# A hybrid decoder step: tensor arithmetic moved off GpSimd, modulation pieces used in pairs, another order at the end of the kernel

## The chip, the cores and the metric

The kernel runs on one NeuronCore of a Trainium2 chip. A core has five engines with queues of their own: TensorE (PE in the profile: matmuls; PEld: its weight loads), VectorE (DVE), ScalarE (ACT), GpSimd (POOL) and SyncE (SP, which here only issues DMAs). Each engine works through its queue in order and waits on semaphores of the others. The metric is the device time of one launch in microseconds (us), median of several runs.

## The reference, cut to what matters

One inference step of a decoder layer, for 256 prompt tokens and 8 sample tokens with states of their own:

```
mod = silu(c) @ w_mod + b_mod                       # 2048 -> 6 x 2048, for 9 conditions
h = rmsnorm(x, g_mix) * (1 + sc_m) + sh_m
u_a, u_b, v_b, z, xbc, dt, gates = split(h @ w_in)
o_a = s5_branch(u_a)         # diagonal complex SSM, scan over tokens, GELU, GLU
o_b = gmlp_branch(u_b, v_b)  # causal 128x128 spatial weights per head, masked
o_c = ssd_branch(z, xbc, dt) # causal conv, Mamba-2 chunked scan with masked scores, gated norm
merged = sum of sigmoid(gate) * (o @ w_p), over a, b, c
x = x + gt_m * (merged @ w_out)
h2 = rmsnorm(x, g_ffn) * (1 + sc_f) + sh_f
up = causal_conv3(h2 @ w_up);  x = x + gt_f * ((silu(up_a) * up_b) @ w_down)
y = rmsnorm(x, g_final)
```

All states at the end of the sequence and of the sample tokens are outputs too.

## The kernel before, in words

Activations lie feature-major: 128 features on the partitions, and T = 264 tokens (256 + 8) in the free dimension. Every weight matrix is streamed from HBM once, in pieces of 512 KB (four k-tiles of 128 by 256 columns, 128x1024 in SBUF). To keep fp32 accuracy, each piece is split (`load_w`, L287): ScalarE rounds it to `hi`, and a subtraction makes the residue `lo` = raw - hi. A gemm of one piece (`gemm_piece`, L308) is 24 matmuls of 128x264: hi by the activation's hi, hi by its lo, and lo by its hi. The residue is made on VectorE, but for some pieces on GpSimd: every third of the first two k-steps (L1130, 6 pieces), and every second of the streams in `SHARED` (L31, L1143: `w_pb`, `w_ga`, `w_pa`, `w_z`, 32 pieces). `raw` has 3 buffers, `hi` and `lo` 4 each; `take` keeps up to three pieces ahead. SP's queue holds all weight loads in order, and the load of a piece waits until the raw buffer's former piece has been read by both engines.

The input projection is done in five k-steps (`KSTEPS`: 2, 2, 4, 4, 4 k-tiles): during each step the modulation of the next one's features is computed (`mod_gen`, L358), since a k-tile can be modulated as soon as its shift and scale are there. Those matmuls use 32 of TensorE's 128 columns each, in one of four column groups (`tile_position`, c = k % 4), and read pieces of 512 KB; in the steps of four k-tiles a piece holds two k's, and the generator loads and uses pieces two at a time. Two consecutive pieces so serve the four column groups.

Work beside the gemms sits in generators: `fill` (S5 preparation and tables, gMLP, SSD), advanced by `pump` by a credit in us for each piece, where each `yield` gives an estimate of the work it emitted, and `mods`, advanced by `mpump`. `finish` drains a generator at once. A planner then orders each engine's instructions by this order of emission and by its own cost model; what is marked high priority goes ahead. On the chip the order of each engine is fixed.

`gen_s5_tables` (L629) builds four tables of cosine and sine by seven doublings each, six GpSimd instructions a doubling; their first reader is the S5 scan (`gen_s5`), which starts at about 340 us. GpSimd also applies three causal or block masks (L781, L948, L1026 to L1030), and issues output DMAs and small DRAM round trips. `rstd_tok` (L490) makes a row of 1/rms for all tokens: three sums, a short chain on VectorE with one square root on ScalarE, three scaled diagonals `dg` on VectorE, and a matmul by ones that broadcasts them to PSUM (`rsb`).

At the end, `residual` (L1331) handles each 256-column group of `w_down`; in the last group each half is squared and summed by its own three matmuls. Then `rstd_tok`, and `final` (L1430) multiplies each piece of the output by the row: some on VectorE from PSUM, some on VectorE and two on GpSimd from a copy in SBUF (`rsb`), and sends it out.

Of the kernel before, what the change touches and what calls it, by code (L numbers as in the profile page):

```python
# [23 lines left out]
NB = 8  # L24
# [6 lines left out]
SHARED = ("w_pb", "w_ga", "w_pa", "w_z")  # L31
# [164 lines left out]
def build(tc, I, O):  # L196
# [62 lines left out]


# [26 lines left out]
    def load_w(src, kk, n, e=V):  # L287
# [5 lines left out]
        sub(lo, raw, hi.bitcast(F32), e)  # L293
# [39 lines left out]
    def mod_part(sec, i, nk, raw):  # L333
        if i == 0:
            mod_ps[sec] = PM("mod")
        ps = mod_ps[sec]
        for j in range(8 // nk):
            k = 8 // nk * i + j
            c = k % 4
            mm(ps[32 * c:32 * c + 32, :128 * nk], cs[:, k, :], raw[:, j, :], k < 4, k >= KD - 4,  # L340
               tile_position=(0, 32 * c))

    def mod_fin(sec, k0, n):
        ps = mod_ps.pop(sec)
# [13 lines left out]
    def mod_gen(s_, k0, nk, depth):  # L358
# [4 lines left out]
        for j in range(len(steps) + depth):  # L363
# [126 lines left out]
    def rstd_tok(pt, PM=PM, n=D):  # L490
# [10 lines left out]
        ts(dg[:, :128], ident, r[:, 0:1], ALU.mult)  # L501
# [127 lines left out]
    def gen_s5_tables():  # L629
        co, si = trig[:, 0], trig[:, 1]  # L630
        tt = W("tt", [P, 512]).rearrange("p (a s m) -> p a s m", a=2, s=4)
        for u in range(4):
            tab = Q1k("tab").rearrange("p (a s t) -> p a s t", a=2, s=4)
            tc_, ts_ = tab[:, 0], tab[:, 1]
            tabs[u] = (tc_, ts_)
            V.memset(tc_[:, :, 0:1], 1.0)
            V.memset(ts_[:, :, 0:1], 0.0)
            e = G
            for b in range(7):
                m = 2 ** b  # L640
                cb = co[:, b, 4 * u:4 * u + 4].unsqueeze(2).to_broadcast([P, 4, m])
                sb = si[:, b, 4 * u:4 * u + 4].unsqueeze(2).to_broadcast([P, 4, m])
# [134 lines left out]
    def gen_gm(ub, vb):  # L777
# [3 lines left out]
        G.affine_select(out=w3, in_=w3, compare_op=ALU.is_ge, fill=0.0, base=0,  # L781
                        pattern=[[0, 8], [1, 128]], channel_multiplier=-1)
# [113 lines left out]
    def gen_ssd(raws):  # L896
# [567 lines left out]
```

## Time and profile before

| | |
|---|---|
| median of 3 runs | 1696.12 us (1695.43 to 1696.61) |
| the profiled execution | 1694.82 us |
| its span, first to last instruction | 1692.8 us |
| mean granted TensorE clock | 0.984 of full speed |
| the chain that ended last | PE 86%, DVE 8%, DMA 2%, ACT 2%, issue 1% |
| DMA | 385.13 MB, mean 228 GB/s |

The busy time of an engine is the union of its instructions' spans; instructions overlap a little in an engine's pipeline, so that the starts of consecutive ones lie closer than their durations. A wait is put down to the producer that came last. The granted clock has two levels, 1.0 (2.4 GHz) and 0.5 (1.2 GHz); a value between is a mean over the stretch. The chain of work that ended last runs through TensorE's gemms for nearly its whole length, so the time is TensorE's work plus the gaps in it.

### The profile page before, as it was taken

The numbers are of one execution on the slowest core, as the hardware profiler recorded it, in microseconds if no ns is written. First come the engines' busy times: TensorE is split into PE (matmuls) and PEld (weight loads), VectorE is DVE, ScalarE is ACT, GpSimd is POOL, SyncE is SP. The second block draws the span as 40 slices with busy tenths as digits, with TensorE's granted clock in tenths as the row PEclk, the third lists the DMA queues.
The fourth block names the chain that finished last, engine by engine and source line by source line (L and its number), as shares of the span: only waits on it lengthen the run. The fifth ranks groups of instructions, "written<-read, shape, count | busy, mean of one in ns | idle before, by whom it ended". The sixth has DMA issues, their size and how long they took to land.

```text
span 1692.8 us, 32239 instructions
## 1 busy us (share of the span) xinstructions
PE 1641.0 (97%) x13175; PEld 1515.9 (90%) x13175; DVE 1098.5 (65%) x1817; ACT 799.7 (47%) x1166; POOL 201.0 (12%) x252
## 2 busy tenths in 40 slices
PE   8999999989988999999999999999999999999996
PEld 6678899877967899879989999999999999999996
DVE  3456877599987658675547666666545566666554
ACT  4423346534345779644335444545333445455442
POOL 0200069133332320000000000000000000000000
PEclk8999999999999999999999999999999999999998
DMA  8867885766477659768996666555555555555552
GB/s 322 299 239 286 339 290 174 284 211 242 174 272 275 224 198 322 258 218 298 337 329 200 229 219 224 175 174 189 184 179 182 180 181 186 178 186 180 186 178 98
DMA packets 107268, 385.13 MB, mean 228 GB/s; under 512 B 12192, under 2 KB 13408, under 8 KB 107120
## 3 DMA queue, kind: packets, MB, share of 16 engines
q1 hardware_dynamic: 103968, 372.58, 63.1%
q0 software_dynamic: 3152, 10.50, 1.7%
q8 instruction: 103, 1.69, 0.4%
q14 instruction: 45, 0.37, 0.1%
HBM read 374.56 MB, written 8.46 MB: 226 GB/s over the span
## 4 chain that ended last, share of the span: by engine, by line
PE 86%; DVE 8%; DMA 2%; ACT 2%; issue 1%; SPq 0%; DVEq 0%; ACTq 0%
PE pg L258 79%; PE mods L258 3%; PE mod L258 2%; DVE lo L243 1%; DVE cv L246 1%; DVE s5b L237 1%; DVE s5gr L737 1%; ACT hi L255 1%; DMA raws<-in_w_mod 1%; DVE s5gi L737 1%; DMA raw<-in_w_pc 0%; DVE s5b L240 0%; DVE s5b L243 0%; PE ypy L258 0%; DMA cT<-in_c 0%
## 5 line engine op out<-in xcount | busy, mean ns | idle before, releaser
L243 DVE TENSOR_TENSOR lo<-raw,hi 128x1024 fp32r<-128x1024 f32 x457 | 568.1, 1244 | 418.6 <-ACT hi L255 401.8
L255 ACT ACTIVATE hi<-raw 128x1024 fp32r<-128x1024 f32 (+1 forms) x495 | 520.4, 1054 | 647.0 <-PE pg L258 495.5
L258 PE MATMUL pg<-hh,hi 128*128 128x264 f32 x1408 | 399.5, 284 | 0.0
L258 PE MATMUL pg<-hh,lo 128*128 128x264 f32 x1408 | 399.3, 284 | 0.0
L258 PE MATMUL pg<-hl,hi 128*128 128x264 f32 x1408 | 398.4, 283 | 0.0
L258 PE MATMUL pg<-xh,hi 128*128 128x264 f32 x1296 | 373.9, 289 | 4.7 <-ACT xh L255 2.5
L258 PE MATMUL pg<-xh,lo 128*128 128x264 f32 x1296 | 369.7, 286 | 1.9 <-DVE lo L243 1.8
L258 PE MATMUL pg<-xl,hi 128*128 128x264 f32 x1296 | 369.0, 285 | 0.0
L258 PEld LDWEIGHTS pg<-xh,hi 128*128 128x128 f32 x1296 | 244.5, 189 | 37.5 <-issue 17.9
L258 PEld LDWEIGHTS pg<-hh,hi 128*128 128x128 f32 x1408 | 264.5, 188 | 10.9 <-issue 9.2
L258 PEld LDWEIGHTS pg<-hl,hi 128*128 128x128 f32 x1408 | 264.4, 188 | 0.0
L258 PEld LDWEIGHTS pg<-hh,lo 128*128 128x128 f32 x1408 | 264.3, 188 | 0.0
L258 PEld LDWEIGHTS pg<-xh,lo 128*128 128x128 f32 x1296 | 243.9, 188 | 8.6 <-issue 4.8
L258 PEld LDWEIGHTS pg<-xl,hi 128*128 128x128 f32 x1296 | 244.4, 189 | 5.2 <-issue 4.9
L258 PE MATMUL pg<-fl,hi 128*128 128x264 f32 x704 | 199.6, 284 | 0.0
L258 PE MATMUL pg<-fh,hi 128*128 128x264 f32 x704 | 199.4, 283 | 0.0
L258 PE MATMUL pg<-fh,lo 128*128 128x264 f32 x704 | 199.3, 283 | 0.0
L258 PEld LDWEIGHTS pg<-fh,hi 128*128 128x128 f32 x704 | 132.4, 188 | 0.0
L258 PEld LDWEIGHTS pg<-fh,lo 128*128 128x128 f32 x704 | 132.4, 188 | 0.0
L258 PEld LDWEIGHTS pg<-fl,hi 128*128 128x128 f32 x704 | 132.3, 188 | 0.0
L243 POOL TENSOR_TENSOR lo<-raw,hi 128x1024 fp32r<-128x1024 f32 x38 | 99.6, 2622 | 274.9 <-ACT hi L255 230.9
L246 DVE SCALAR_TENSOR_TENSOR fcv<-pg,par,fcv 128x255 f32<-128x255 f32 (+1 forms) x176 | 83.9, 477 | 1.5 <-ACT fcv L255 1.5
(346 smaller groups left out, 1990.9 us busy)
## 6 DMA issues: line engine op xcount, KB each, us to landing
raw<-in_w_up SPq DMA_DIRECT2D x176, 512.0 KB, 3.5
raws<-in_w_mod SPq DMA_DIRECT2D x128, 512.0 KB, 5.9
raw<-in_w_down SPq DMA_DIRECT2D x88, 512.0 KB, 3.5
raw<-in_w_a SPq DMA_DIRECT2D x64, 512.0 KB, 5.2
rawm<-in_w_m SPq DMA_DIRECT2D x64, 512.0 KB, 7.0
raw<-in_w_ga SPq DMA_DIRECT2D x32, 512.0 KB, 3.8
raw<-in_w_gc SPq DMA_DIRECT2D x32, 512.0 KB, 5.0
raw<-in_w_out SPq DMA_DIRECT2D x32, 512.0 KB, 4.6
```

Source lines behind the costliest of these rows:

```text
L237: e.tensor_tensor(o, a, b, op=ALU.mult)
L243: e.tensor_tensor(o, a, b, op=ALU.subtract)
L246: V.scalar_tensor_tensor(o, a, s, b, op0=op0, op1=op1)
L255: S.activation(o, a, f, **kw)
L258: TE.matmul(o, l, r, start=start, stop=stop, skip_group_check=True, **kw)
L737: V.tensor_tensor_scan(g[:, s, k], rb, b[:, s, k], ini[:, 4 + r, s:s + 1] if c else 0.0, op0=ALU.mult, op1=ALU.add)
```

## The change

- `load_w` always makes the residue on VectorE; `SHARED` and the choice of engine are gone.
- `gen_s5_tables` does cosine and sine in one instruction each time, four instructions a doubling in place of six, on VectorE; the estimates given to `pump` go from 0.2 a doubling to 0.7 to 1.7 (6.7 a table).
- The masks become products with `tri` on VectorE; the masked scores `CB` are read from PSUM by that product, so ScalarE's copy goes. In the decode part the block matrix `E` and its eight matmuls are replaced by two small products with strided columns of `ident` and two matmuls by `ones` in two column groups.
- `mod_gen` uses the two pieces of a pair in the reverse order of their loading; `mod_part` counts per column group which matmul is the first and the last, since the order is no longer that of k.
- `rstd_tok` makes the first of the three diagonals on ScalarE.
- In the last group the two squares are added on VectorE and summed by three matmuls once. Twelve matmuls of 256 columns on zeros, whose result nobody reads, are queued behind them. The output is sent in eight parts, with five multiplications and two fused ones on VectorE that read the row in PSUM, and two on GpSimd.

```diff
-    def load_w(src, kk, n, e=V):
+    def load_w(src, kk, n):
...
-        sub(lo, raw, hi.bitcast(F32), e)
+        sub(lo, raw, hi.bitcast(F32))
...
     def mod_part(sec, i, nk, raw):
-        if i == 0:
-            mod_ps[sec] = PM("mod")
-        ps = mod_ps[sec]
+        if sec not in mod_ps:
+            mod_ps[sec] = PM("mod"), [0] * 4
+        ps, seen = mod_ps[sec]
         for j in range(8 // nk):
             k = 8 // nk * i + j
             c = k % 4
-            mm(ps[32 * c:32 * c + 32, :128 * nk], cs[:, k, :], raw[:, j, :], k < 4, k >= KD - 4,
+            seen[c] += 1
+            mm(ps[32 * c:32 * c + 32, :128 * nk], cs[:, k, :], raw[:, j, :], seen[c] == 1, seen[c] == KD // 4,
                tile_position=(0, 32 * c))
...
-                for p_, raw in enumerate(got.popleft()):
+                for p_, raw in reversed(list(enumerate(got.popleft()))):
                     mod_part(sec, i + p_, nk, raw)
...
-        ts(dg[:, :128], ident, r[:, 0:1], ALU.mult)
+        act(dg[:, :128], ident, AF.Copy, scale=r[:, 0:1])
...
-                t1, t2 = tt[:, 0, :, :m], tt[:, 1, :, :m]
-                mult(t1, ts_[:, :, :m], sb, e)
-                mult(t2, ts_[:, :, :m], cb, e)
-                mult(tc_[:, :, m:2 * m], tc_[:, :, :m], cb, e)
-                mult(ts_[:, :, m:2 * m], tc_[:, :, :m], sb, e)
-                sub(tc_[:, :, m:2 * m], tc_[:, :, m:2 * m], t1, e)
-                add(ts_[:, :, m:2 * m], ts_[:, :, m:2 * m], t2, e)
-                yield 0.2
+                t, new = tt[:, :, :, :m], tab[:, :, :, m:2 * m]
+                mult(t, tab[:, :, :, :m], sb)
+                mult(new, tab[:, :, :, :m], cb)
+                sub(new[:, 0], new[:, 0], t[:, 1])
+                add(new[:, 1], new[:, 1], t[:, 0])
+                yield (0.7, 0.7, 0.7, 0.8, 0.9, 1.2, 1.7)[b]
...
-        G.affine_select(out=w3, in_=w3, compare_op=ALU.is_ge, fill=0.0, base=0,
-                        pattern=[[0, 8], [1, 128]], channel_multiplier=-1)
+        mult(w3, w3, tri.unsqueeze(1).to_broadcast([P, 8, 128]))
...
-        act(CB, pt.rearrange("p (c g i) -> p c g i", c=2, g=2), AF.Copy)
-        CBf = CB.rearrange("p c g i -> p (c g) i")
-        G.affine_select(out=CBf, in_=CBf, compare_op=ALU.is_ge, fill=0.0, base=0,
-                        pattern=[[0, 4], [1, 128]], channel_multiplier=-1)
+        mult(CB.rearrange("p c g i -> p (c g) i"), pt.rearrange("p (c i) -> p c i", c=4),
+             tri.unsqueeze(1).to_broadcast([P, 4, 128]))
...
-        for t in range(8):
-            mm(pe[:, 16 * t:16 * t + 16], E[:16, 128 * t:128 * t + 128], ddf, True, True)
+        for o in range(2):
+            mm(pe[64 * o:64 * o + 64, :128], ones[:16, :64], ddm[:, o].rearrange("p t c -> p (t c)"), True, True,
+               tile_position=(0, 64 * o))
...
-                if end:
-                    sum_tok(sst[0], [t[:, 0, :]], False, j0 == 1)
+                if not end:
+                    add(ssq, ssq, t)
+                elif j0 == 0:
+                    t0 = t
                 else:
-                    add(ssq, ssq, t)
+                    add(t, t, t0)
+                    sum_tok(sst[0], [t[:, 0, :]], False, True)
...
+    wps = PG()
+    with tc.issue_after(newest(TE)):
+        for _ in range(12):
+            mm(wps[:, 0, :256], wsrc[:, :128], wsrc, True, True)
     rs = rstd_tok(sst[0])
+    rsb = W("rsb", [P, T])
+    act(rsb, rs, AF.Copy)
...
     final(0, h0, rs, V)
-    rsb = W("rsb", [P, T])
-    act(rsb, rs, AF.Copy)
     final(1, h0, rsb, G)
     final(0, h1, rs, V)
-    final(2, slice(0, 4), rsb, V)
+    final(2, h0, rs, V)
+    final(2, h1, rs, V)
     final(1, h1, rsb, G)
-    mult(x1[3][:, h0, :], x1[3][:, h0, :], rsb.unsqueeze(1).to_broadcast([P, 2, T]))
-    for j in (2, 3):
-        stt(x1[3][:, j, :], x1[3][:, j, :], pv("g_final", 12 + j, 13 + j), rsb, ALU.mult, ALU.mult)
-    nc.sync.dma_start(O["y"][3], x1[3])
+    final(3, h0, rs, V)
+    final(3, h1, rs, V, True)
```

## Rows read from the trace of the kernel before

**Rows 1.** The page's busy time of each engine: us, share of the span, instructions

```profile
PE 1641.0 (97%) x13175; PEld 1515.9 (90%) x13175; DVE 1098.5 (65%) x1817; ACT 799.7 (47%) x1166; POOL 201.0 (12%) x252
```

**Rows 2.** TensorE's waits: waiting group, releaser, us in total, times, longest

```profile
PE rsb L258 <- DVE dg L250: 8.9, 2, 7.0
PE mods L258 <- DMA raws<-in_w_mod: 5.6, 4, 3.8
...
PE pg L258 <- ACT xh L255: 2.5, 1, 2.5
```

**Rows 3.** Windows: us, busy time by engine, TensorE's clock, DMA share, GB/s

```profile
60.00:70.00 10.00, 7.49 (x42) 4.53 (x41) 7.81 (x14) 4.69 (x8) 2.46 (x1) 0.83 0.94 327
...
180.00:190.00 10.00, 10.00 (x81) 8.04 (x81) 9.93 (x38) 3.19 (x4) 0.00 (x0) 1.00 1.02 391
...
215.00:297.00 82.00, 82.00 (x677) 80.81 (x676) 61.02 (x95) 43.17 (x50) 72.70 (x168) 1.00 0.69 232
297.00:340.00 43.00, 43.00 (x367) 37.35 (x359) 22.54 (x38) 22.18 (x30) 8.16 (x6) 1.00 0.79 282
...
335.00:560.00 225.00, 207.23 (x1581) 172.54 (x1580) 195.84 (x331) 97.66 (x151) 72.16 (x32) 0.95 0.66 239
```

**Rows 4.** GpSimd's residues, groups of instructions, 335 to 560 us

```profile
L243 POOL TENSOR_TENSOR lo<-raw,hi 128x1024 fp32r<-128x1024 f32 x25 | 68.3, 2732 | 147.1 <-ACT hi L255 134.4 <-PE mods L258 12.7
```

**Rows 5.** Timeline of VectorE and GpSimd: start us, us, engine, line, instruction

```profile
30.00 0.17 DVE L237 TENSOR_TENSOR hd<-hd,rstd 128x16 f32<-128x16 f32 x1
...
61.14 2.35 DVE L237 TENSOR_TENSOR hd<-x,gs 128x16 f32<-128x16 f32 x1
...
106.30 0.42 DVE L243 TENSOR_TENSOR lo<-raw,hi 128x256 fp32r<-128x256 f32 x1
...
334.53 0.28 DVE L237 TENSOR_TENSOR s5d<-h0s,a_i 128x128 f32<-128x128 f32 x1
...
344.40 2.40 POOL L243 TENSOR_TENSOR lo<-raw,hi 128x1024 fp32r<-128x1024 f32 x1 [5.04 <-PE mods L258]
344.46 0.70 DVE L237 TENSOR_TENSOR acc<-acc,pg 128x528 f32<-128x528 f32 x1
345.07 2.27 DVE L240 TENSOR_TENSOR s5b<-s5b,s5gi 128x512 f32<-128x512 f32 x1
347.26 0.68 DVE L243 TENSOR_TENSOR s5b<-s5b,s5gr 128x512 f32<-128x512 f32 x1
...
556.09 2.41 DVE L240 TENSOR_TENSOR cv<-cv,pre 128x32 f32<-128x32 f32 x1
```

**Rows 6.** VectorE's residues of whole pieces, 215 to 297 and 730 to 890 us

```profile
L243 DVE TENSOR_TENSOR lo<-raw,hi 128x1024 fp32r<-128x1024 f32 x27 | 35.5, 1315 | 9.7 <-ACT hi L255 9.7
...
L243 DVE TENSOR_TENSOR lo<-raw,hi 128x1024 fp32r<-128x1024 f32 x47 | 57.5, 1224 | 49.9 <-ACT hi L255 48.0 <-PE mods L258 1.6
```

**Rows 7.** Windows of TensorE, modulation matmuls alone: busy (records), clock, DMA

```profile
60.00:112.00 52.00, 16.68 (x68) 0.97 0.69 249
...
157.00:215.00 58.00, 8.10 (x64) 1.00 0.84 309
```

**Rows 8.** Timeline: a broadcast at 889 us, and the end

```profile
889.20 0.71 PE L258 MATMUL rsb<-dg,ones 128*128 128x264 f32 x2
...
1680.72 0.62 DVE L250 TENSOR_SCALAR dg<-ident,rtk 128x128 f32<-128x128 f32 x3
1681.40 1.25 PE L258 MATMUL rsb<-dg,ones 128*128 128x264 f32 x2 [1.95 <-DVE dg L250]
1682.68 0.70 DVE L237 TENSOR_TENSOR x<-x,rsb 128x528 f32<-128x528 f32 x1 [1.34 <-PE rsb L258]
...
1683.85 4.18 DVE L237 TENSOR_TENSOR x<-x,rsb 128x528 f32<-128x528 f32 x3 [0.46 <-ACT rsb L255]
1687.96 0.88 DVE L246 SCALAR_TENSOR_TENSOR x<-x,par,rsb 128x264 f32<-128x264 f32 x2
```

**Rows 9.** Timeline of TensorE: the decode expansion

```profile
624.69 1.95 PE L258 MATMUL dde<-dd,E 16*128 16x16 f32 x16
```

More of the change, by code (lines that the diff above doesn't have):

```diff
@@ L30 @@
 BRK = None
-SHARED = ("w_pb", "w_ga", "w_pa", "w_z")
 NFF = 44
@@ L258, in mm, with newest @@
         TE.matmul(o, l, r, start=start, stop=stop, skip_group_check=True, **kw)
+    def newest(e):
+        return next(i for i in reversed(nc.cur_bb.bb.instructions) if i.engine == e.engine)
     ident = cst.tile([P, P], F32, name="ident")
@@ L1024, in gen_ssd_dec @@
         dd, bc, yv = xsb["dd"], xsb[2], xsb["yv"]
-        E = Q1k("E")
-        G.memset(E[:16, :], 1.0)
-        G.affine_select(out=E[:16, :], in_=E[:16, :], compare_op=ALU.is_ge, fill=0.0, base=0,
-                        pattern=[[1, 1024]], channel_multiplier=-64)
-        G.affine_select(out=E[:16, :], in_=E[:16, :], compare_op=ALU.is_ge, fill=0.0, base=63,
-                        pattern=[[-1, 1024]], channel_multiplier=64)
+        ddm = W("ddm", [16, 2, 8, 2 * NB])
+        ddf = dd.rearrange("p a b -> p (a b)")
+        for o in range(2):
+            mult(ddm[:, o], ddf.unsqueeze(1).to_broadcast([16, 8, 2 * NB]),
+                 ident[:16, o:16:2].unsqueeze(2).to_broadcast([16, 8, 2 * NB]))
         yield BRK
         pe = PM("dde")
-        ddf = dd.rearrange("p a b -> p (a b)")
-        for t in range(8):
-            mm(pe[:, 16 * t:16 * t + 16], E[:16, 128 * t:128 * t + 128], ddf, True, True)
+        for o in range(2):
+            mm(pe[64 * o:64 * o + 64, :128], ones[:16, :64], ddm[:, o].rearrange("p t c -> p (t c)"), True, True,
+               tile_position=(0, 64 * o))
         dx = cst.tile([P, 8, 2, NB], F32, name="dx")
@@ L1129, in build @@
             n = 128 if gs == [DT] else 256 * len(gs)
-            e = G if (i % 2 == 1 if nk == 1 else i % 3 == 1 and nk == 2) else V
-            queue.append((I[f"w_a{s_}"][o:o + P * nk * n].rearrange("(p n) -> p n", p=P), nk, n, e))
+            queue.append((I[f"w_a{s_}"][o:o + P * nk * n].rearrange("(p n) -> p n", p=P), nk, n))
             o += P * nk * n
@@ L1142, in stream @@
         for i in lead_order(I[name].shape[0]) if name == "w_up0" else range(I[name].shape[0]):
-            e = G if i % 2 == 1 and name in SHARED else V
-            queue.append((I[name][i], nk, 256, e))
+            queue.append((I[name][i], nk, 256))
     for name in ("w_gb", "w_pb", "w_ga", "w_pa", "w_z", "w_gc", "w_pc", "w_out", "w_up0", "w_down0", "w_up1", "w_down1"):
@@ L1166, in build @@
     wps = PG()
-    wsrc = W("wsrc", [P, 256], BF16)
+    wsrc = cst.tile([P, 256], BF16, name="wsrc")
     V.memset(wsrc, 0.0)
@@ L1427, in build, with final @@
                 lambda k: (AH[(k + p0) // 4][:, k % 4, :], AL[(k + p0) // 4][:, k % 4, :]), np_, 8, epi_d, 0)
+    wps = PG()
+    with tc.issue_after(newest(TE)):
+        for _ in range(12):
+            mm(wps[:, 0, :256], wsrc[:, :128], wsrc, True, True)
     rs = rstd_tok(sst[0])
-    def final(q, js, r, e):
+    rsb = W("rsb", [P, T])
+    act(rsb, rs, AF.Copy)
+    def final(q, js, r, e, lone=False):
         v = x1[q][:, js, :]
         n = v.shape[1]
-        mult(v, v, r.unsqueeze(1).to_broadcast([P, n, T]), e=e)
+        if lone:
+            for j in range(js.start, js.stop):
+                stt(x1[q][:, j, :], x1[q][:, j, :], pv("g_final", 4 * q + j, 4 * q + j + 1), r, ALU.mult, ALU.mult)
+        else:
+            mult(v, v, r.unsqueeze(1).to_broadcast([P, n, T]), e=e)
         nc.sync.dma_start(O["y"][q].rearrange("p (j t) -> p j t", j=4)[:, js, :], v)
```

14 lines of the change are left out of this document (6 added, 8 removed).

## The prediction

> **What bounds the kernel now.** I read the engines' shares first, then TensorE's waits, then windows, then single instructions of VectorE and GpSimd. The shares [rows 1] show a TensorE program: it is busy 1641.0 of 1692.8 us, so a faster VectorE is worth nothing by itself. What can be won is the 51.8 us in which TensorE is idle, the stretches in which it runs at the lower clock after such a gap, and matmuls that take more of its time than they need.
>
> TensorE's waits [rows 2] name the ends of small chains (a diagonal, a modulated input, a weight piece of the modulation), none of which names GpSimd. The windows [rows 3] say where: between 335 and 560 us TensorE is busy 207.2 of 225 us at a mean granted clock of 0.95, so 17.8 us are idle, and 0.05 of 225 us, 11 us, is what the lower of the two clock levels takes there; I put 8 us of it on busy time, the rest falls in the gaps. VectorE is busy 195.8 us in that window. Yet VectorE at its limit is not enough to stop TensorE: between 180 and 190 us it is busy 9.93 of 10 us and TensorE 10.00 [rows 3]. In that earlier stretch GpSimd does nothing.
>
> That leads to single instructions [rows 5]. A subtraction on VectorE of 128x512 takes 0.68 us at 347.26 us; the addition of the same size at 345.07 us, begun while a residue runs on GpSimd (344.40 to 346.80 us), takes 2.27 us and ends 0.54 us after GpSimd. The multiplication just before it, at 344.46 us, also fell into that residue, but reads one operand from PSUM and took its usual 0.70 us. From 335 to 560 us GpSimd runs 25 residues of 2.73 us [rows 4], and 24 VectorE instructions are prolonged in this way, the first and the last being the one at 345.07 us and the one at 556.09 us (2.41 us; a small one takes 0.17). The excess over the undisturbed twin, summed over the 24, is 44 us. It happens in front of whatever VectorE has next, which is often the residue that TensorE needs. At 61 us it is `hd`, an instruction of 0.17 us that took 2.35, and TensorE stood 2.51 us for the `xh` behind it [rows 2, 5].
>
> GpSimd's table instructions do much less of it: in 215 to 297 us, where they fill GpSimd for 72.7 us [rows 3], the 27 residues on VectorE average 1.315 us against 1.224 us later [rows 6], 2.5 us in all.
>
> The Trainium skill ("SBUF — State Buffer", section "Who interferes with whom") says that a VectorE instruction with two SBUF inputs and a GpSimd instruction that reads SBUF exclude each other for the whole instruction, and that one with at most one SBUF input is not touched. The trace agrees with both halves (2.27 for 0.68 us, and 0.70 us as usual). It speaks for c and for the end below, and against hoping for much from moving the tables: by the rule each short instruction can hold VectorE only for its own short time.
>
> **The change, part by part.** The sum is made against the profiled execution, 1694.8 us (span 1692.8 and 2.0 around it); that is 1.3 us under the median of the runs, so the differences are then taken from 1696.1.
>
> *a) Residues of the first two k-steps to VectorE (6 of them).* The stall of `hd` goes (2.2 us), and with the 2.5 us gap most of the low clock behind it: 60 to 70 us has clock 0.83 [rows 3], 1.7 us lost, part of it inside the gap. Three residues of 1.22 us come into VectorE there, in a stretch where it waits for ScalarE anyway. The weights are also coming in nearly as fast as they ever do there, so some is given back. Value -2.5; bounds 0 and -4.
>
> *b) Modulation pieces in pairs.* With four k-tiles a step, a piece holds two k-tiles and so uses two of TensorE's four column groups; a pair uses all four at once. Between 157 and 215 us pairs stay together: 64 matmul records in 8.10 us. Between 60 and 112 us most were pulled apart by gemm matmuls: 68 records take 16.68 us [rows 7], where 68/64 of 8.10 is 8.6. That is 8.1 us of TensorE's time in a stretch without idle, about 1 us of it from the low clock counted in a. Issuing the later-loaded piece first makes one wait for both, so nothing can be put between them. The new wait: TensorE stands until the second piece has landed, and all gemm matmuls queue behind it. Before, TensorE never waited for these pieces, so they had landed by then; going faster eats that slack. Value -5; bounds -8 and +1 (one late landing).
>
> *c) The 32 shared residues to VectorE.* In 335 to 560 us VectorE loses 44 us of stalls and takes on 25 residues of 1.224 us [rows 6], 30.6 us: 195.8 becomes 182, against the 225 - 17.8 - 8 = 199 us that TensorE needs there without gaps and low clock. So VectorE falls from 98% of what TensorE needs to 92%, and the 2 us bursts that hit the queue at random go. Against it: those residues used a queue of their own and now stand behind the S5 and convolution arithmetic; and in `w_pa`, the last 40 us of the stretch, one piece brings VectorE a residue (1.22), two evacuations (0.70 each [rows 5]) and 2.2 us of fill credit, 4.8 us, where TensorE's 24 matmuls take 2.9, so it stays full there even without stalls. The raw slots come free earlier (1.2 for 2.7 us), which helps the 5.6 us of waits for modulation weights [rows 2] as far as SP's queue, which carries them too, stands on those slots. Of 17.8 + 8 = 26 us I take half: -13; bounds -26 and -3 (the lower end if only the net 13 us of VectorE counted and three quarters of it were hidden).
>
> *d) S5 tables to VectorE.* 4 tables of 7 doublings of 4 instructions. By undisturbed durations [rows 5, 6], a doubling costs 2x0.68+2x0.42 at the top, 2x0.42+2x0.28 below it, then about 1.0 (between the rows of 128 and 16 elements) and 0.8, and about 0.7 for each of the three smallest: 7.4 us a table, 29.6 in all; starts lie some 0.08 us closer than durations, so 21 is the lower end. With the mask of the spatial weights (1.2 us) less the 2.5 us of held residues, 215 to 297 us asks 61.0 + 28.3 = 89 of 82 us [rows 3]. The 7 us over spill into 297 to 340 us, where 20 us are free, before the tables' first reader at about 340. TensorE has up to three pieces ready, 3 x 24 matmuls at 82/677 us [rows 3], 8.7 us, so most is covered. If the cover is gone, the 7 us and a few of low clock show. Value +2; bounds 0 and +8.
>
> *e) The end.* Today: diagonal 0.62 us, broadcast matmul 1.25 us at the lower clock, then VectorE from 1682.68 to 1688.84 [rows 8], of which three multiplications took 4.18 us beside GpSimd's two. After: the five multiplications read the factor from PSUM, the form that kept its 0.70 us beside GpSimd at 344 us [rows 5] and has it at 1682.68 us, and the two last are 0.88 us together: 5 x 0.62 (start to start) + 0.88 = 4.0 for 6.2 us, -2.2. One third of the diagonal on ScalarE: -0.2. The 12 warming matmuls let the broadcast run in 0.71 us as at 889 us: -0.5, or, if the clock falls all the same, they run at half speed in front of it: +0.6. The sum of the last two squares costs an addition (0.42) and saves six matmul records beside it: 0. Two more output DMAs, smaller ones; all of the output still has to flow, in less time than before, which may give 1 us back; I take 0.4. Value -2.2 - 0.2 - 0.5 + 0.4 = -2.5; bounds -0.5 and -3.5.
>
> *f) Decode expansion.* 16 matmul records, 1.95 us [rows 9], become 4 of about 0.27: -1.4 (bounds 0, if the two new VectorE products come late, and -1.5). The masked scores are one VectorE instruction for ScalarE's copy and GpSimd's mask, with VectorE free a third of the time there: 0. GpSimd's queue keeps only DMA issues and two multiplications; they start no earlier than their data, so 0. The 7.0 us wait of the SSD norm's broadcast [rows 2] hangs on ScalarE and DMA, and stays but for 0.2 us.
>
> Sum: -2.5 - 5 - 13 + 2 - 2.5 - 1.4 = -22.4; 1696.1 - 22.4 = 1673.7, and I say **1673**.
>
> **The rivals.**
> *All of it (0.08).* VectorE's bursts were the only cause from 335 to 560 us and every pair closes up: -4 - 8 - 26 + 0 - 3.5 - 1.4 = -43: 1653. For it: 180 to 190 us. Against it: convolution and `w_pa`, where VectorE is full also without GpSimd.
> *The queue, not the stalls (0.20).* TensorE's gaps come from residues that stand behind fill work in VectorE's order, and 25 more stand there now; c gives -3: total -12, 1684. For it: VectorE is still over 90% used. Against it: again 180 to 190 us, where VectorE had every residue.
> *VectorE becomes the bound (0.07, slower).* One in-order queue now carries tables, residues and S5. If TensorE's lead is used up at about 280 us, the 7 us excess and the low clock after it cost 10 us. And from 335 to 560 us VectorE was idle for 225 - 195.8 = 29 us: if the stalls mostly took such idle time, only 44 - 29 = 15 us of them counted, and 30.6 us of residues come for them, +15.6 on VectorE; half of it on TensorE's path makes c +8. Together -2 - 3 + 10 + 8 - 2.5 - 1.4 = +9: 1705. It decides where VectorE holds a residue back for longer than the three pieces of TensorE's lead last. For it: VectorE is busy 87% of that window already. Against it: 180 to 190 us.
> *Pairs do not close up (inside the forecast's range).* If the wait on the later piece is placed as before, b is 0 and the time 1679.
>
> **How the numbers follow.** The forecast has 0.62, its own range 1663 to 1682; the last 0.03 lie within 0.2% of 1696, which is what a measurement can tell from no change. The range 1657 to 1690 takes in the forecast and the second rival and leaves out some 0.17. Faster: 0.62 + 0.08 + 0.20 = 0.90; same 0.03; slower 0.07.
>
> **What would show it.** No VectorE instruction of 128x512 over 1 us from 335 to 560 us, and TensorE's idle there under 10 us: c right. Modulation records only in eights from 60 to 112 us, about 9 us in all: b right. TensorE busy 10 of 10 us from 222 to 300 us with VectorE near 10: d right; a gap there is the third rival. A broadcast matmul of 0.7 us and no multiplication over 0.75 us on VectorE at the end: e right. It is wrong if the idle from 335 to 560 us stays near 18 us with the stalls gone.

## The result, and the profile after

The changed kernel takes 1657.1 us, median of 4 runs (1656.0 to 1662.77), beside 1696.05 us for the kernel before (1695.43 to 1696.61): a ratio of 0.9777, 95% interval 0.9754 to 0.98. That is 39 us less, where the forecast was 23 less (1673); it is faster, as forecast. The median lies below the forecast's own 1663 to 1682 us, and inside the whole range of 1657 to 1690 by 0.1 us, which is luck: two of its four runs took less than 1657. The profiled execution took 1656.0 us, its span 1654.3.

The page's engine shares after, to read beside [rows 1]:

```profile
PE 1619.4 (98%) x13163; PEld 1506.8 (91%) x13163; DVE 1097.2 (66%) x1969; ACT 802.5 (49%) x1170; POOL 21.1 (1%) x41
```

VectorE took over GpSimd's arithmetic, but for two multiplications of the output, and is busy no longer than before (1097.2 against 1098.5 us). It took on 38 residues of 1.22 us and 29.9 us of tables, and yet the durations of its instructions add up to only 11 us more (1205.8 for 1194.5): most of what it took on, it had lost before in prolonged instructions. TensorE is busy 21.6 us less and idle 34.9 instead of 51.8 us. Its waits after (waiting group, releaser, us in total, times, longest), beside [rows 2]:

```profile
PE rsb L257 <- DVE dg L249: 8.7, 3, 6.8
PE mod L257 <- DMA rawm<-in_w_m: 3.0, 1, 3.0
...
PE mods L257 <- DMA raws<-in_w_mod: 2.4, 1, 2.4
```

The wait for `xh` at 62 us is gone; a wait of 3.0 us for a modulation piece (`rawm`) is new. The windows after, beside [rows 3] (us, busy time of PE, PEld, DVE, ACT, POOL, clock, DMA share, GB/s):

```profile
60.00:70.00 10.00, 10.00 (x82) 7.89 (x85) 6.31 (x8) 2.12 (x2) 0.00 (x0) 1.00 0.98 372
...
215.00:297.00 82.00, 80.33 (x667) 78.06 (x665) 69.62 (x161) 40.80 (x46) 0.85 (x1) 1.00 0.63 214
...
335.00:560.00 225.00, 220.98 (x1759) 189.03 (x1759) 192.66 (x380) 113.47 (x167) 4.37 (x8) 0.99 0.75 265
```

From 335 to 560 us TensorE is idle for 4.0 instead of 17.8 us and its clock is 0.99 instead of 0.95; 1759 matmul records fit into the window instead of 1581. VectorE's instructions there, by group and then in time, beside [rows 5, 6]:

```profile
L242 DVE TENSOR_TENSOR lo<-raw,hi 128x1024 fp32r<-128x1024 f32 x58 | 70.6, 1218 | 19.0 <-ACT hi L254 12.3 <-PE mods L257 6.4
L236 DVE TENSOR_TENSOR s5b<-s5b,tab 128x512 f32<-128x512 f32 x14 | 9.0, 685 | 0.0
```

```profile
345.64 1.22 DVE L242 TENSOR_TENSOR lo<-raw,hi 128x1024 fp32r<-128x1024 f32 x1
346.77 0.68 DVE L242 TENSOR_TENSOR s5b<-s5b,s5gi 128x512 f32<-128x512 f32 x1
347.38 0.68 DVE L239 TENSOR_TENSOR s5b<-s5b,s5gr 128x512 f32<-128x512 f32 x1
```

Each 128x512 takes 0.68 us, each residue 1.22; the addition of 2.27 us has no successor. TensorE's modulation matmuls alone, beside [rows 7] (busy, records, clock, DMA):

```profile
60.00:112.00 52.00, 10.84 (x72) 0.97 0.84 316
...
157.00:215.00 58.00, 8.52 (x64) 1.00 0.91 323
```

72 records now take 10.84 us, where 68 took 16.68. The end of the kernel, beside [rows 8] (lines of TensorE, VectorE, ScalarE and SP together), and the decode expansion, beside [rows 9]:

```profile
590.52 0.43 PE L257 MATMUL dde<-ddm,ones 16*64 16x128 f32 x4
...
1641.12 1.77 PE L257 MATMUL pg<-wsrc 128*128 128x256 bf16 x12
1643.10 1.22 PE L257 MATMUL rsb<-dg,ones 128*128 128x264 f32 x2 [0.22 <-DVE dg L249]
...
1644.78 3.16 DVE L236 TENSOR_TENSOR x<-x,rsb 128x528 f32<-128x528 f32 x5 [1.82 <-ACT rsb L254]
1647.86 0.88 DVE L245 SCALAR_TENSOR_TENSOR x<-x,par,rsb 128x264 f32<-128x264 f32 x2
...
1644.36 0.39 ACT L254 ACTIVATE rsb<-rsb 128x264 f32<-128x264 f32 x1 [1.43 <-PE rsb L257]
...
1646.16 4.48 SPq L1443 DMA_DIRECT2D out_y<-x  x8
```

The broadcast still takes 1.22 us, and the first output leaves only at 1646.16.

**Where the 38.5 us of span went.** The table has TensorE's stage lengths in us, from the first matmul of one stage to that of the next. The other columns are the experiments of the next section, `again` being the changed kernel once more.

| stage | before | after | again | shared_pool | twin_one | twin_four | first_pool | no_reverse | first_and_order | tables_pool |
|---|---|---|---|---|---|---|---|---|---|---|
| start to the first gemm | 31.2 | 26.1 | 26.0 | 27.0 | 28.8 | 28.4 | 29.1 | 26.8 | 29.4 | 26.3 |
| to `gms` (spatial matmuls) | 270.1 | 263.4 | 264.7 | 261.9 | 262.8 | 262.0 | 261.7 | 267.6 | 270.1 | 261.2 |
| `w_pb` to the transposes after `w_pa` | 233.5 | 211.4 | 210.4 | 233.3 | 250.6 | 248.7 | 211.3 | 214.5 | 210.2 | 211.7 |
| to the decode expansion `dde` | 55.2 | 54.9 | 54.0 | 55.3 | 60.9 | 61.6 | 54.0 | 54.0 | 54.0 | 54.9 |
| `dde` to the SSD norm's sums `css` | 90.7 | 87.7 | 92.5 | 90.3 | 92.3 | 87.7 | 91.4 | 91.0 | 92.7 | 94.7 |

So 11.7 us came before `gms`, none from there to `w_pb` (34.7 us in every run), 22.2 from `w_pb` to the end of `w_pa`, 3.3 up to `css`, 1.1 from there to the last gemm, and 0.3 at the end. The 3.0 us from `dde` to `css` cannot be put down to the change: again, the same kernel, needs 92.5 us there and so more than before. At `gms` the executions of kernels that are the same up to there lie at 288.2 (end_order), 289.5 (after), 290.7 (again) and 291.4 us (end_free), so one execution's time there is good to 1 or 2 us. Much of this arises before the first gemm, which begins at 25.9, 26.1, 26.0 and 28.5 us in these four. At 22 us the same 32 modulation matmuls take 1.93 us in the first profile after and 3.64 us in end_free, at a granted clock of 1.00 and 0.50.

### The profile page after: what moved, and what is told of

Read it like the earlier page. It is cut to its first block, busy times and chain, and to the rows that moved or that the text cites. A ratio compares the mean times of both kernels' runs of the same rounds, so it can differ in the third digit from the quotient of the medians.

```text
span 1654.3 us, 32132 instructions
## 1 busy us (share of the span) xinstructions
PE 1619.4 (98%) x13163; PEld 1506.8 (91%) x13163; DVE 1097.2 (66%) x1969; ACT 802.5 (49%) x1170; POOL 21.1 (1%) x41
## 4 chain that ended last, share of the span: by engine, by line
PE 58%; issue 3%; DMA 2%; DVE 1%; ACT 1%; POOL 0%; SPq 0%; DVEq 0%; POOLq 0%; ACTq 0%
PE pg L257 55%; PE mods L257 2%; DMA out_ssm_s<-hst 1%; DMA raw<-in_w_gc 1%; DMA raw<-in_w_pc 0%; ACT hi L254 0%; DVE lo L242 0%; PE sst L257 0%; PE rsb L257 0%; DVE x L245 0%; DVE x L236 0%; DVE hst L239 0%; POOL out_ssm_s L1070 0%; POOL BC L1049 0%; ACT rsq L254 0%
## 5 line engine op out<-in xcount | busy, mean ns | idle before, releaser
L242 DVE TENSOR_TENSOR lo<-raw,hi 128x1024 fp32r<-128x1024 f32 (+1 forms) x495 | 601.8, 1217 | 412.7 <-ACT hi L254 392.3
L257 PEld LDWEIGHTS pg<-hh,hi 128*128 128x128 f32 x1408 | 264.5, 188 | 10.9 <-issue 9.2
L257 PE MATMUL pg<-mh,hi 128*128 128x264 f32 x256 | 73.1, 285 | 0.0
```

The lines of the kernel that those rows point to most:

```text
L242: e.tensor_tensor(o, a, b, op=ALU.subtract)
L257: TE.matmul(o, l, r, start=start, stop=stop, skip_group_check=True, **kw)
```

## The experiments

The theory: VectorE's instructions with two SBUF operands were held by GpSimd's, and that is where most of the time was (c, and a at the beginning). The rivals: it is the order in VectorE's queue, or something else in the change. The kernels below are the changed kernel with the edit shown.

**shared_pool: the 32 shared residues back on GpSimd.**

```diff
-        sub(lo, raw, hi.bitcast(F32))
+        sub(lo, raw, hi.bitcast(F32), e)
...
+            e = G if i % 2 == 1 and name in SHARED else V
```

> The changed kernel with the residues of every second piece of w_pb, w_ga, w_pa and w_z on GpSimd again, 32 of them. Theory (GpSimd's residues hold VectorE, and TensorE stands for it): the 22 us that the changed kernel gained between the first S5 matmul and the convolution come back nearly whole, 1657 + 20 = 1677 us (1670 to 1682), with some 24 VectorE instructions prolonged by about 1.8 us each. Rival (the gain there came from weights that arrive earlier, or from the planner's new order): within 5 us of 1657.

Measured: 1681.0 us (1677.33 to 1682.46), ratio 0.9908 (0.989 to 0.9925). Its window, and GpSimd's residues in it:

```profile
335.00:560.00 225.00, 205.95 (x1581) 173.74 (x1580) 196.08 (x334) 98.22 (x147) 70.40 (x31) 0.96 0.67 242
...
L243 POOL TENSOR_TENSOR lo<-raw,hi 128x1024 fp32r<-128x1024 f32 x25 | 69.0, 2762 | 147.8 <-ACT hi L255 129.6 <-PE mods L258 18.2
```

This is the window of before again [rows 3, 4], to 1.3 us of TensorE's busy time, and the stage is 233.3 us long, as before (210.2 to 214.5 in the kernels that leave these residues on VectorE and add nothing to GpSimd there). All of the 22 us in that stage are the shared residues.

**twin_one: does being held cost, or having the residues elsewhere?** All residues stay on VectorE. At each of the 32 places GpSimd makes a subtraction of 128x928 of two SBUF operands as well, whose result nobody reads.

```diff
         sub(lo, raw, hi.bitcast(F32))
+        if twin:
...
+            m = 928 // 1
+            for q in range(1):
+                c = slice(m * q, m * q + m)
+                sub(scr[:, c], xf[:, c], hf[:, c], G)
```

> The changed kernel, all residues on VectorE, and for the same 32 pieces GpSimd subtracts a 128x928 part of the new hi from an old tile into a scratch that nobody reads. Theory (being held is what costs): VectorE gets some 40 us of stalls on top of 193 us of work in the 225 us of that stretch, more than it has, so +20 to +40: 1677 to 1697 us. Rival (what cost was the lateness of residues made on GpSimd, 2.7 us for 1.2, or raw buffers held for longer): nothing waits for GpSimd here, so 1657 within 3 us.

Measured: 1706.14 us (1700.99 to 1708.5), ratio 1.0055 (1.0036 to 1.0074). Its window, and groups of it:

```profile
335.00:560.00 225.00, 200.68 (x1476) 165.45 (x1469) 206.94 (x332) 85.24 (x135) 71.50 (x29) 0.92 0.65 228
...
L243 DVE TENSOR_TENSOR lo<-raw,hi 128x1024 fp32r<-128x1024 f32 x46 | 65.4, 1426 | 14.0 <-PE mods L258 8.7 <-ACT hi L255 5.2
...
L237 DVE TENSOR_TENSOR s5gr<-s5b,tab 128x512 f32<-128x512 f32 x7 | 8.7, 1247 | 0.0
...
L243 POOL TENSOR_TENSOR scr<-xh,hi 128x928 fp32r<-128x928 f32 x23 | 68.2, 2967 | 145.4 <-ACT hi L255 124.6 <-ACT s5po L704 17.6 <-ACT s5b L703 3.2
```

Work that nobody waits for cost some 47 us (the difference of the two ratios, 0.0278, of 1696), 1.5 us for each of 32 instructions of 2.93 us, more than the upper end expected. VectorE has the same instructions, but the multiplication of 0.68 us averages 1.25. The whole gain of the change is gone, and more, though GpSimd's results are read by nobody. GpSimd also reads `hi` here and could hold that buffer for longer; but no wait of TensorE, VectorE or ScalarE in this trace names GpSimd, and SP's only one is for the output at the end. The rival falls.

**twin_four: is it the length of GpSimd's instruction?** The tables on GpSimd had held VectorE little [rows 6], and the prediction put that down to their short instructions. Here the same unread subtraction is cut into four of 128x232.

```diff
+            m = 928 // 4
+            for q in range(4):
+                c = slice(m * q, m * q + m)
+                sub(scr[:, c], xf[:, c], hf[:, c], G)
```

> As the kernel with the unread subtractions on GpSimd, but each of the 32 is cut into four of 128x232. Theory (GpSimd holds VectorE only until its running instruction ends, so short instructions hold little, as the table instructions did): less than half of what the whole ones cost, 1662 to 1682 us. Rival (what counts is GpSimd's total time on two SBUF operands): as with whole ones, 1695 to 1710 us.

Measured: 1700.33 us (1696.35 to 1704.28), ratio 1.0038 (1.0023 to 1.0053). The theory that short ones hold little falls; the time is the rival's. Eight of them side by side with VectorE (start us, us, engine, instruction):

```profile
392.94 1.30 DVE L243 TENSOR_TENSOR lo<-raw,hi 128x1024 fp32r<-128x1024 f32 x1
394.17 1.17 DVE L237 TENSOR_TENSOR s5gr<-s5b,tab 128x512 f32<-128x512 f32 x1
395.26 1.16 DVE L237 TENSOR_TENSOR s5gi<-s5b,tab 128x512 f32<-128x512 f32 x1
396.35 2.25 DVE L237 TENSOR_TENSOR s5b<-s5b,tab 128x512 f32<-128x512 f32 x2
...
391.51 9.81 POOL L243 TENSOR_TENSOR scr<-xh,hi 128x232 fp32r<-128x232 f32 x8 [7.99 <-ACT s5po L704]
```

The two engines take turns, one instruction each: every VectorE instruction of 0.68 us lasts 0.49 us longer, and each of GpSimd's 1.2 us (the shortest in this run are 0.67). The prediction was right that one short instruction holds VectorE only for its own short time, and wrong in what it drew from that. What counts, to judge by these rows, is how many VectorE instructions with two SBUF operands stand back to back while GpSimd has work. Where the tables were, in the kernel before, VectorE had one long residue now and then, with PSUM additions and pauses between:

```profile
233.66 1.30 POOL L240 TENSOR_TENSOR tab<-tab,tt 128x64 f32<-128x64 f32 x1
...
233.55 1.23 DVE L243 TENSOR_TENSOR lo<-raw,hi 128x1024 fp32r<-128x1024 f32 x1 [0.72 <-ACT hi L255]
235.03 0.70 DVE L240 TENSOR_TENSOR acc<-acc,pg 128x528 f32<-128x528 f32 x1 [0.26 <-PE pg L258]
```

There GpSimd waited (1.30 us for an instruction that takes 0.32 alone) and VectorE did not. That explanation is read from these rows; no run here tried other work beside the tables.

**first_pool, no_reverse, first_and_order: the opening, singly and together.** Six residues of the first k-steps back on GpSimd; the pieces of a pair in the order of their loading; both.

```diff
+            e = G if i % 3 == 1 and nk == 2 else V
...
-                for p_, raw in reversed(list(enumerate(got.popleft()))):
+                for p_, raw in enumerate(got.popleft()):
```

> The changed kernel with the six residues of the first two k-steps on GpSimd again. Theory: the first one holds the last sum of squares at 13 us (2.2 us, and TensorE then stays at the lower clock for longer, together 5 us before the first gemm), another holds the sample tokens' modulation between the first two steps (2 to 3 us): 1664 us (1661 to 1667). Rival (the start gained from the diagonal on ScalarE and from buffers): 1657 within 2 us.

> The changed kernel with the two pieces of a pair used in the order of loading. Theory: the planner again puts gemm matmuls between the two in the second and third k-step, modulation records in fours there, 5 to 8 us more of TensorE's time: 1663 us (1661 to 1666). Rival (pairs close up by themselves once the residues are on VectorE): 1657 within 2 us.

> The changed kernel with two parts undone at once: the six residues of the first two k-steps back on GpSimd, and the pieces of a pair used in the order of their loading. The spatial matmuls (gms) start at 301.2 us before and at 289.5 to 291.4 us with the change; undone singly the two parts moved them by 1.3 us (residues) and 4.9 us (order), which with the 2 us that the tables cost there leaves some 8 us of the 11.7 unexplained. Theory: the two cover for each other, each leaving slack in the stream of weights that hides the other's absence; undone together they cost 10 to 13 us there: gms at 300 to 303 us, time 1667 to 1670. Rival: they add up, 6.2 us, and the rest lies in other parts of the change: gms at 295 to 297.5 us, time 1663 to 1665.

Measured: first_pool 1660.61 us (1659.18 to 1661.47), ratio 0.979 (0.9775 to 0.9805), between its two expectations; no_reverse 1663.21 (1659.92 to 1666.62), ratio 0.98 (0.9781 to 0.9818), as expected; first_and_order 1672.66 (1669.72 to 1673.45), ratio 0.9869 (0.9853 to 0.9886), beyond what either side expected. Against the first profile after, `gms` moves by 1.3 us (290.8), 4.9 us (294.4), and with both by 10.0 us (299.5, just under the 300 to 303 of the theory). Against the mean of the four executions named above (290.0) it is 0.9, 4.5 and 9.5; first_pool alone lies within their spread. Either way the two do not add up, and the rival of 295 to 297.5 falls. The medians say the same: by the ratios the three are some 2, 4 and 16 us above the changed kernel. TensorE's modulation matmuls alone, as above, in no_reverse:

```profile
60.00:112.00 52.00, 14.60 (x63) 1.00 0.73 269
```

And in first_and_order:

```profile
60.00:112.00 52.00, 15.56 (x68) 1.00 0.72 257
```

The pairs are pulled apart again in both. Where the excess arises can be read by following one and the same gemm matmul through the traces. The table has its delay against the first profile after, in us; the columns are the times at which it starts in that profile.

| | 45.0 | 65.1 | 91.8 | 125.3 | 260.0 | 280.2 |
|---|---|---|---|---|---|---|
| before | 4.4 | 9.3 | 15.3 | 12.3 | 13.4 | 11.7 |
| first_pool | 2.9 | 3.1 | 3.1 | 2.7 | 2.7 | 1.3 |
| no_reverse | 0.1 | 1.8 | 7.8 | 4.8 | 4.8 | 4.9 |
| first_and_order | 2.6 | 6.0 | 12.0 | 9.0 | 10.2 | 10.0 |
| end_free | 2.1 | 2.1 | 2.1 | 2.5 | 2.5 | 1.9 |

The new wait at 92 us (2.96 us, in the waits above) is not where lost time is made up: first_pool and end_free are about as late behind it as ahead of it, and first_pool stands 3.61 us there. With the pairs apart the wait is gone, and no_reverse and first_and_order each get 3.0 us back. The excess of first_and_order arises between 45 and 65 us, where the wait for `xh` is back, and by 1.1 us between 125 and 260 us; and first_pool makes up 1.4 us between 260 and 280 us, where its gap before the gMLP norm is 0.31 us long instead of 1.67. The two waits, of first_pool and of first_and_order:

```profile
98.97 0.56 PE L257 MATMUL pg<-xh,hi 128*128 128x264 f32 x1 [3.61 <-DVE acc L239]
```

```profile
63.34 0.51 PE L257 MATMUL pg<-xh,hi 128*128 128x264 f32 x2 [2.53 <-ACT xh L254]
```

So with the pairs closed the residues on GpSimd cost nothing behind the first gemm, and with the pairs apart some 2.8 us there (the growth from 45 to 260 us of first_and_order's delay over that of no_reverse). That the two together cost more than their sum is measured; why closed pairs shield TensorE from these residues is not shown, and each row is one execution.

**tables_pool: the S5 tables back on GpSimd**, in the six instructions a doubling of before.

```diff
-                mult(t, tab[:, :, :, :m], sb)
...
+                mult(t1, ts_[:, :, :m], sb, e)
```

> The changed kernel with the S5 tables on GpSimd again, six instructions a doubling. Theory (part d cost 2 us at the broadcast of the gMLP norm at 275 us, and the tables' short instructions hold VectorE for 2.5 us in all, beside its waits for ScalarE): 1655 to 1657 us, no wait over 0.5 us at that broadcast. Rival (tables on GpSimd cost as the residues did): 1662 us and more.

Measured: 1659.98 us (1655.04 to 1666.41), ratio 0.9799 (0.9758 to 0.984): inconclusive by the time. In the trace the theory's sign is there: TensorE's gap before that broadcast is 0.04 us, and 0.04 in tables_end below, for 1.67, 1.49, 1.12 and 0.28 us in after, again, end_free and end_order, which have the tables on VectorE. `w_pb` begins at 322.1 instead of 324.2 us, but in end_order at 322.9; `dde` to `css` then took 94.7 us. The same pair without GpSimd's part at the end, tables_end and end_free, has `w_pb` at 323.9 and 326.1 us, 2.2 apart, of which 1.2 are there already at the first gemm. So of the 2 us at `w_pb` only what the gap holds can be put down to the tables.

**end_order, best, end_free, tables_end, again: the end.** end_order puts the first multiplication ahead of ScalarE's copy. best adds to it 18 unread matmuls ahead of the sums and high priority for two norms. end_free, from the changed kernel, makes all nine multiplications on VectorE from PSUM, with no copy, and has the 18 matmuls too. tables_end is end_free with the tables on GpSimd. again has no edit.

end_order:

```diff
     rs = rstd_tok(sst[0])
-    rsb = W("rsb", [P, T])
-    act(rsb, rs, AF.Copy)
...
     final(0, h0, rs, V)
+    rsb = W("rsb", [P, T])
+    act(rsb, rs, AF.Copy)
```

> The changed kernel, only with the first output multiplication ahead of the copy of the row to SBUF. Theory: the first output leaves about 1 us earlier (6.9 to 7.1 us after the last gemm matmul in place of 8.1), and as the output flows without a gap from then on, the end moves with it: -1 us, 1656 us. Rival (the end is set by VectorE's last multiplication): no change of the time from the last gemm to the end.

best, in addition (the second edit at both norms):

```diff
                     add(t, t, t0)
+                    if scale:
+                        wp1 = PG()
+                        with tc.issue_after(newest(TE)):
+                            for _ in range(18):
+                                mm(wp1[:, 0, :256], wsrc[:, :128], wsrc, True, True)
...
-        ps = rstd_tok(pt, n=1024)
+        with tc.high_priority():
+            ps = rstd_tok(pt, n=1024)
```

> The changed kernel, with three additions: the first output multiplication ahead of the copy of the row to SBUF (1 us at the end, since SP's queue gets its first output earlier), 18 more unread matmuls between the last gemm and its sum of squares, so that TensorE does not stand idle there (the broadcast in 0.7 for 1.2 us, 0.5 us), and high priority for the two norms in the gMLP and SSD branches, whose square root stood behind ScalarE's next rounding (the wait of 6.9 us at the SSD norm falls to about 3, the one of 1.7 us at the gMLP norm to under 0.5). Sum -6: 1651 us. Rival (the wait at the SSD norm is set by its data, not by ScalarE's order): 1655 us.

end_free, with the first of best's two edits:

```diff
     rs = rstd_tok(sst[0])
-    rsb = W("rsb", [P, T])
-    act(rsb, rs, AF.Copy)
...
-    final(1, h0, rsb, G)
+    final(1, h0, rs, V)
...
-    final(1, h1, rsb, G)
+    final(1, h1, rs, V)
```

> Only the end of the changed kernel is edited: all nine multiplications of the output on VectorE from PSUM, no copy on ScalarE, nothing on GpSimd, and 18 more unread matmuls ahead of the sums so that the clock is still up at the broadcast. Theory: the end failed because the first output DMA waited (8.08 us after the last gemm): at half clock for the broadcast, then for the copy, then for the GpSimd piece that stands first in the queue of SP; from there the output flows at some 390 GB/s and needs 8.1 us to the last instruction. Without these three the first output DMA is issued some 6.4 us after the last gemm and the last instruction ends 14.6 us after it instead of 16.2; time 1.6 us under that of the unedited kernel beside it. Rival: an earlier first output gains nothing, since VectorE's last multiplication sets the end (0.6 us for each multiplication, seven of them and two fused ones, 5.1 us); then 16.0 to 16.4 us after the last gemm, and the time is the same.

> The end as in end_free, and the S5 tables on GpSimd again in their old form of six instructions a doubling. Theory: on VectorE the tables cost TensorE 2 us in front of w_pb (322.1 against 324.2 us in the kernel with the tables on GpSimd), since GpSimd's short instructions do not hold VectorE's few long residues there; the gain stays, and the kernel is 2 us under end_free, 3.6 us under the unedited one: 1653 (1651 to 1655). Rival: VectorE's bursts are only moved, and what is won at w_pb is lost again to the weights by w_up (as 5 us were between the decode expansion and css in one run): within 1 us of end_free.

> The changed kernel once more, nothing edited, beside the next two kernels on the same chip: it shows how far one profiled execution stands from another. Time 1657 us (1655 to 1661). From the decode expansion to the fused decode state (dde to css) the kernels with the change took between 87.7 and 94.7 us although nothing in that stage differs between them. If that is a difference from execution to execution, this one, too, lies apart from the 87.7 us of the first profile by 2 us or more (89 to 93); if the 87.7 us belong to the kernel's own order of instructions, it takes 87.7 again within 0.7.

Measured: end_order 1659.06 us (1652.62 to 1662.09), ratio 0.9788 (0.9757 to 0.982); best 1656.46 (1654.62 to 1659.41), 0.978 (0.9754 to 0.9806); end_free 1658.03 (1655.81 to 1660.74), 0.9785 (0.9765 to 0.9804); tables_end 1656.52 (1652.44 to 1662.33), 0.9777 (0.9753 to 0.9802); again 1659.29 (1657.73 to 1660.09), 0.979 (0.9772 to 0.9808). By the time none is told apart from the changed kernel; best missed its 1651, end_order its 1656 and tables_end its 1653. The stage from `dde` to `css` took 92.5 us in again, inside the 89 to 93 that were expected if it differs from execution to execution. The traces tell the ends apart, counted from the end of the last gemm matmul:

| | before | after | again | end_order | best | end_free |
|---|---|---|---|---|---|---|
| first output DMA issued, us | 7.0 | 8.1 | 7.6 | 7.0 | 6.5 | 6.5 |
| last instruction of the span, us | 16.4 | 16.2 | 15.7 | 16.2 | 15.7 | 14.6 |

end_free met its 6.4 and 14.6. Its last VectorE instruction ends 10.9 us after the last gemm, later than in the changed kernel (10.7), and yet its span ends 1.6 us sooner: the rival, that VectorE's last multiplication sets the end, falls. The end of its trace, TensorE, VectorE and SP:

```profile
1649.47 0.68 PE L257 MATMUL rsb<-dg,ones 128*128 128x264 f32 x2 [0.52 <-DVE dg L249]
...
1650.19 4.39 DVE L236 TENSOR_TENSOR x<-x,rsb 128x528 f32<-128x528 f32 x7 [0.87 <-PE rsb L257]
...
1650.93 4.82 SPq L1446 DMA_DIRECT2D out_y<-x  x8
...
1654.50 0.88 DVE L245 SCALAR_TENSOR_TENSOR x<-x,par,rsb 128x264 f32<-128x264 f32 x2
```

end_order shows why an earlier first output alone is not enough. SP then waited 1.4 us for GpSimd's piece in its queue, and the flow of the output had holes (windows of end_order, columns as before, the last two the DMA share and GB/s):

```profile
1649.00:1650.00 1.00, 0.00 (x0) 0.00 (x0) 1.00 (x3) 0.00 (x0) 1.00 (x2) 0.50 0.56 218
1650.00:1651.00 1.00, 0.00 (x0) 0.00 (x0) 1.00 (x3) 0.00 (x0) 1.00 (x1) 0.50 0.33 127
1651.00:1652.00 1.00, 0.00 (x0) 0.00 (x0) 0.78 (x2) 0.00 (x0) 0.05 (x1) 0.50 1.03 393
```

High priority for the norms gained nothing that shows: the wait at the SSD norm is 7.0 us in best, where 3 were expected. Its chain was cut by a table load and a gate on ScalarE (square root at 687.38, diagonal at 689.40 us; 684.27 and 685.31 after), and `w_out` begins no earlier than the spread of that stage allows to tell.

## Why the prediction was right in sign and short in size

**The bound.** Right: TensorE is the bound before and after, and the gain came from its gaps, its clock and the matmuls pulled apart. Neither of the slower or smaller rivals came: *The queue* needed the idle from 335 to 560 us to stay (4.0 us are left), and *VectorE becomes the bound* falls on TensorE's 220.98 of 225 us in the same window. The nearest is *All of it* (1653), which was given 0.08. The span fell by 16 us more than the sum: 9 of them are c, 6 the opening (11.7 for the 5.5 of a, b and d together) and 3 the stages from the end of `w_pa` to the last gemm (4.4 for the 1.4 of f), and the end gave 2 less.

**c, the step that was mis-sized: -13 forecast, -22 measured** (233.5 to 211.4 us, undone alone 233.3). The mechanism was as written; the halving of the 26 us was what failed. It rested on VectorE staying full in `w_pa` without GpSimd too, 4.8 us a piece where TensorE's matmuls take 2.9. The window of before, and of after, over `w_pa` and the first pieces of `w_z`:

```profile
519.00:569.00 50.00, 44.40 (x334) 39.65 (x333) 45.02 (x76) 32.47 (x45) 18.62 (x11) 0.93 0.72 255
```

```profile
492.00:535.00 43.00, 42.52 (x335) 36.94 (x334) 39.90 (x77) 30.19 (x42) 2.72 (x5) 1.00 0.93 319
```

Nearly the same matmuls (334 and 335 records) took 7 us less, and TensorE is busy 42.52 of 43 us beside a VectorE that is busy 93%. For `w_pa` alone, 491.9 to 521.0 us in the trace after, eight pieces take 29.1 us, 3.6 each with the modulation matmuls among them; VectorE is busy 27.9 of these, 3.5 a piece and not 4.8, and TensorE all of them. So VectorE was full there, as forecast, but at less work a piece, and it did not hold TensorE up. The forecast that VectorE would fall to 182 us of 225 failed: VectorE is busy 192.66 us, since with TensorE faster more work lies in the window (380 instructions for 331, 58 residues). The Trainium skill ("SBUF — State Buffer", section "Who interferes with whom") calls the two engines' use of the shared port an exclusive lock for the whole instruction; the trace of twin_four agrees (1.17 us for 0.68, in turns).

**a and b: -2.5 and -5 forecast, -10.0 together measured at `gms`.** Both mechanisms are there (TensorE 10.00 us of 10 from 60 to 70 us at clock 1.00; 10.84 us of modulation, not the 9 forecast, since the matmuls behind the gap at 92 us begin at the lower clock and one group of eight is split there). b has its size, 4.9 us undone alone. The terms were added as if independent, and they are not: undone alone a costs 1.3 us, on top of b 5.1. The new wait of b, "one late landing", came at 2.96 us. The start before the first gemm was not forecast at all: 5.1 us. GpSimd's first residue held the addition of squares of the very first norm, before and after:

```profile
13.59 2.85 DVE L240 TENSOR_TENSOR sq<-sq 128x528 f32<-128x528 f32 x1
...
13.23 2.65 POOL L243 TENSOR_TENSOR lo<-raw,hi 128x1024 fp32r<-128x1024 f32 x1 [11.60 <-ACT hi L255]
```

```profile
13.62 0.70 DVE L239 TENSOR_TENSOR sq<-sq 128x528 f32<-128x528 f32 x1
```

The matmuls that sum these squares begin at 14.38 us after, at 16.49 before and at 16.57 in first_pool: some 2 us are the residue's. The first gemm begins at 29.1 us in first_pool, 3.1 later than after, but at up to 28.8 us in kernels without that residue, so the 3.1 cannot be read as its price. Ahead of the gMLP norm's gap, at 260 us in the table of delays, the change is 13.4 us ahead of before, and a and b undone take back 10.2 of them. Of the rest, 1.8 are there at 45 us. The rows of before have 12 unread matmuls between those sums and the modulation, in a stretch in which TensorE does not pause from 16.49 to 26.0 us; in the changed kernel all unread matmuls of the start lie ahead of the sums:

```profile
19.08 2.72 PE L258 MATMUL pg<-wsrc 128*128 128x256 bf16 x12
```

No run put them back, so that this is their part in the 1.8 us is likely and not shown; the rest stays open.

**d: +2 forecast, +0.2 to +1.6 measured** (the gap that both kernels with the tables on GpSimd lack). The tables take 29.9 us of VectorE, as forecast; a table's terms add up to 7.5 us, not the 7.4 written. Where d shows was not foreseen. TensorE has its gap at 274.54 to 276.21 us, before the broadcast of the gMLP norm, whose chain on VectorE stood behind table products and a residue (VectorE, then TensorE):

```profile
273.04 1.22 DVE L242 TENSOR_TENSOR lo<-raw,hi 128x1024 fp32r<-128x1024 f32 x1
274.18 0.42 DVE L242 TENSOR_TENSOR tab<-tab,tt 128x256 f32<-128x256 f32 x1
274.51 0.42 DVE L239 TENSOR_TENSOR tab<-tab,tt 128x256 f32<-128x256 f32 x1
274.85 0.17 DVE L500 RECIPROCAL rtk<-rtk 128x3 f32<-128x3 f32 x1
...
276.21 0.68 PE L257 MATMUL rsb<-dg,ones 128*128 128x264 f32 x2 [1.67 <-DVE dg L249]
```

So it is a latency of a small chain, not the 7 us of excess work; from 215 to 297 us TensorE has no other gap over 0.25 us.

**e: -2.5 forecast, -0.3 measured in the first profile and -0.8 in that of again; the step that failed.** VectorE's part came out as written: from the first multiplication to the last 3.96 us (forecast 4.0) for 6.16. But the last VectorE instruction no longer sets the end. From the first output DMA on, 8 x 264 KB flow at some 390 GB/s, 5.5 us, and 8.1 us pass from the issue to the last instruction. That issue came later than before, counted from the last gemm (8.1 for 7.0 us): the first multiplication waited for the copy that the change had moved ahead of it, and GpSimd's piece stands first in SP's queue. "All of the output still has to flow" stood in the prediction, as a small credit instead of the bound. With the twelve matmuls alone the clock stayed up in three of ten executions (again, twin_one, tables_pool: broadcast 0.68 us, span's end 15.7 us after the last gemm) and fell in seven (1.1 to 1.2 us, 16.2; the granted clock of 1643 to 1644 us is 0.50 in the first profile). With 18 more ahead of the sums, in best, end_free and tables_end, the broadcast took 0.68 us each time.

**f: -1.4 forecast.** The rows agree (1.95 to 0.43 us); the stage around it differs by 4.8 us between two executions of the same kernel, so the time cannot show it.

**The 7 us wait of the SSD norm** stayed, as forecast: 6.8 us (7.0 before).

## What to carry to other kernels

Look at single instructions of VectorE that last longer than their twins, and count them back to back beside GpSimd: work on GpSimd that nobody waits for can cost half of its own duration on the critical path, and cutting it into four helped little here. Two gains in one stretch of the same stream of weights need not add up; undo both at once to see. At the end of a kernel ask when the first byte of the output can leave and whether the pieces then follow without holes, in the order of the queue that sends them, not when the last arithmetic is done.

## What the runs showed of the hardware that was not expected

GpSimd and VectorE take turns instruction by instruction on two SBUF operands: 0.68 became 1.17 us beside instructions of 128x232, and GpSimd's own averaged 1.13 us, where the shortest took 0.67. A GpSimd instruction can be the one that waits (1.30 us for 0.32). Two executions of the same kernel differed by 4.8 us in one stage (87.7 and 92.5 us), in which weights, states in and states out share the DMA queues and SP stands for some 20 us behind the states written out; the cause of the difference was not tried.
